# The turning ahead of the second half's rows, at 3 units of the schedule for a tile instead of 5.5

## The chip, the cores and the metric

The kernel runs on one core of one Trainium2 chip. The metric is the device time of one execution in microseconds (us), as the median of three runs. One core has five engines with queues of their own: PE (matrix products), DVE and ACT (vector and scalar work on tiles of 128 partitions), POOL (a second vector engine) and SP, which here only issues DMAs. Each engine works through its own instructions in the order in which the program was built; an instruction waits at the head of its queue until what it needs is there.

## The reference

One layer of a decoder trunk, for a prompt of 2048 tokens of width 1024 and eight single tokens with states of their own:

- rows are normalised by their root mean square and modulated by a learned scale and shift, `hn = rmsnorm(x) * (1 + scale) + shift`;
- one projection `z = hn @ w_in` yields the columns of two groups of heads;
- the first group (RG-LRU) runs a convolution of width 4, two block-diagonal gates, and a linear recurrence along the tokens, times `silu(za)`;
- the second (GLA, 4 heads) runs gated linear attention in chunks, a norm for each head, times `silu(zg)`;
- both are joined, projected by `w_out`, gated, added to `x`, and normalised once more.

The result is the output rows and the new states. All is float32; the kernel writes an operand as a high and a low part (`hh`, `hl` for the activations) and sums three products, so each projection of 1024 inputs is 24 matmuls (8 steps of lines L683, L684, L685).

## The kernel before, in words

The prompt is worked in two halves of 1024 tokens. In the first half the kernel projects and processes the heads of both groups; meanwhile it prepares what the second half needs, so that this work lies beside the matmuls. One such preparation is `turn_ahead` (L245 to L269). For each of the 8 tiles of 128 rows of the second half it

1. loads the rows to a tile `x` (SP, L248);
2. sums their squares (ACT, L166, called `squares`);
3. takes the root in 12 small steps on DVE (`scales`, lines L148 to L154) and multiplies the rows by it (`times`, L182, DVE);
4. turns the tile in blocks of 32x32 into a second tile `w` (DVE, L257);
5. stores `w` to a scratch in DRAM, `xtd` (SP, L261), and goes on to the next tile.

`x` and `w` are both tiles named `xt`, of which two slots exist. The rows come back later through `hn_load` (L271, DMAs at L281): group 0 (256 tokens) to two more tiles `xt`, groups 1 to 3 to `xst`. `modulate` (L188) then makes the new `hh` and `hl` from them: ACT at L201, DVE at L203, POOL at L204 for the high part, DVE at L205 for the low one. `modulate` runs bit by bit between the last matmuls of the first half.

The order is written by a small scheduler. `tick(u)` advances a clock by u units, where the main program calls it after each projection (one unit is a projection of 512 tokens, 24 matmuls); `after(u, f)` asks for f to be called when u more units have passed. What f issues then stands at that place in each engine's queue. The framework that builds the program gives out the slots of tiles and sets the semaphores by the order in which instructions come.

Behind the first half stands `gates_ahead` (L1662), the first user of the new rows. It loads two tiles of weights `w_6208` and `w_6210` (L315, 1 MB each) and projects with each of them tokens 0 to 255, then 256 to 511, then 512 to 1023 of the new half; the results go to PSUM tiles `acc`, of which there are four slots. A result leaves PSUM by ACT at L1152 (a sigmoid) and DVE at L1153, and then its slot is free. In the same stretch the last gate products of the recurrence stand (L1338 to L1340, `acc_6359` and `acc_6364`), and on DVE the sums of blocks for a seven-product scheme (`sums`, L1512, L1515, L1516, L1521).

Other names: `on` is the output of an attention head, which DVE scales at L1112 (four pieces) before PE transposes it at L1186; `vl` at L980 is the low part of a head's values, and frees the PSUM tile it reads; L1090 to L1098 are the products of an attention chunk; L327 on DVE splits weights.

Of the kernel before, what the change touches and what calls it, by code (L numbers as in the profile page):

```python
# [54 lines left out]
def hybrid_kernel(ctx, tc, i, o):  # L55
    nc = tc.nc
    V, S, G, PE, SP = nc.vector, nc.scalar, nc.gpsimd, nc.tensor, nc.sync
# [110 lines left out]
    def squares(pool, xt, m=P, tag="f512", ss=None, j0=0):  # L168
        if ss is None:
            ss = pool.tile([P, 4], F32, tag="ss", name="ss", bufs=2)  # L170
        for j, x in enumerate(xt, j0):
            square_sum(pool, ss[:m, j:j + 1], x[:m], m, D, tag)
        return ss

    def scales(pool, ss, n, m=P):
        rs = pool.tile([P, 4], F32, tag="rs", name="rs", bufs=2)
        rsqrt(pool, rs[:m, :n], ss[:m, :n], n, m, 1.0 / D)
        return rs

    def times(xt, rs, m=P, j0=0):  # L180
        for j, x in enumerate(xt, j0):
            V.tensor_scalar(x[:m], x[:m], rs[:m, j:j + 1], None, op0=OP.mult)  # L182
# [62 lines left out]
    def turn_ahead(q):  # L245

        x, w = [xp.tile([P, TH + NS], F32, tag="xt", name="xt")[:, :D] for _ in range(2)]
        SP.dma_start(x, i["x_prompt"][0, TH + q * P:TH + (q + 1) * P])  # L248

        def scaled(ss):  # L250
            with behind(V):
                times([x], scales(xp, ss, 1))
            after(0.5, turned)

        def turned():
            with behind(V):
                V.transpose(w.rearrange("p (c k j) -> p c k j", c=4, k=KT), x.rearrange("p (k c j) -> p c k j", c=4, k=KT))  # L257
            after(0.5, stored)

        def stored():  # L260
            SP.dma_start(xtd[q], w)  # L261
            if q < 7:
                after(1, lambda: turn_ahead(q + 1))

        def squared():
            ss = squares(xp, [x])
            after(0.5, lambda: scaled(ss))

        after(3, squared)  # L269

    def hn_load(g):  # L271

# [430 lines left out]
    def behind(q):  # L703

        return tc.issue_after(next(x for x in reversed(list(nc.cur_bb.bb.instructions)) if x.engine == q.engine))
# [17 lines left out]
    def after(units, fn, gla=False, val=False):  # L723
        clock[1] += 1
        heapq.heappush(pend, (clock[0] + units, clock[1], fn, gla, val))
# [17 lines left out]
    def ada_gate():  # L743

        pg = acc()

        def step(kt):
            ws = [xp.tile([P, TH + NS], F32, tag="xt", name="xt")[:, :D] for _ in range(2)]
            for n, w in enumerate(ws):
                SP.dma_start(w, i["w_ada"][0, (kt + n) * P:(kt + n + 1) * P, 2 * D:])  # L750

            def mm():
                for n in (1, 0):
                    for g in range(4):
                        PE.matmul(pg[32 * g:32 * g + 32, :256], sc[:, kt + n], ws[n][:, g * 256:(g + 1) * 256],
                                  start=kt == 0 and n == 1, stop=kt == KT - 2 and n == 0)
                if kt + 2 < KT:
                    step(kt + 2)
                else:
                    gr = xp.tile([P, 512], F32, tag="f512", name="gr")[:, :256]  # L760
                    S.copy(gr, pg[:, :256])
                    SP.dma_start(gated, gr)
                    after(4, lambda: ready("gate"))
                    turn_ahead(0)
            after(3, mm)

        step(0)
# [1512 lines left out]
```

## Time and profile before

| | |
|---|---|
| median of 3 runs | 1453.05 us (1452.84 to 1454.38) |
| the profiled execution | 1451.16 us, span 1449.4 us |
| mean granted TensorE clock | 0.993 |
| instructions | 23539 |
| PE busy | 1412.9 us, 97% of the span |
| DVE, ACT, POOL busy | 1064.7, 693.2, 221.1 us |
| the 8 turns L257 on DVE | 225.1 to 571.3 us, 1.24 us each |
| the 8 stores L261 on SP | 226.3 to 572.5 us |

Times inside the profile are counted from the start of the span. A row of a timeline gives the start, the duration, the engine, the line, the operation and its tiles; a figure in brackets is the idle time of that engine ahead of the row, with what ended it. Matmuls are pipelined, so the distance of two starts, and not the duration of one, is the pace.

### The profile page before, as it was taken

Reading aid. Unit: us, or ns where it says so; the run is one execution under the profiler, and the core shown is the slowest. Engines: PE = TensorE matmul, PEld = TensorE weight load, DVE = VectorE, ACT = ScalarE, POOL = GpSimd, SP = SyncE. Lnnn points to the kernel's source line nnn. Section 1 sums busy time; section 2 is a strip of 40 time slices with the busy share of each in tenths; the row PEclk is TensorE's granted clock in tenths of the full one; section 3 lists DMA queues with packets and bytes.
Section 4 is the critical chain, followed back from the end, with each engine's and each line's share of the span. In section 5 each row is a group of like instructions: output and inputs, shape, how many; then the busy total and the mean of one; then the engine's idle time right before and its main releaser. Section 6 shows DMA issues by size and latency. Waiting matters only on the chain.

```text
span 1449.4 us, 23539 instructions
## 1 busy us (share of the span) xinstructions
PE 1412.9 (97%) x8677; PEld 1244.8 (86%) x8677; DVE 1064.7 (73%) x2529; ACT 693.2 (48%) x1259; POOL 221.1 (15%) x366
## 2 busy tenths in 40 slices
PE   7999999999999998899999999999999999999998
PEld 6889989888898987788899999999998887778886
DVE  5757668777777687945448688596888986688886
ACT  4644544563456357624444554535567522144342
POOL 1200111122121113200110432333210000000000
PEclk9999999999999999899999999999999999999999
DMA  9755776875676646677744675665671767694453
GB/s 331 265 185 175 263 246 220 285 263 185 199 241 219 220 169 190 212 247 237 280 165 148 203 247 163 231 198 187 239 253 68 283 227 276 223 356 139 137 166 116
DMA packets 166424, 313.71 MB, mean 216 GB/s; under 512 B 13410, under 2 KB 94978, under 8 KB 163869
## 3 DMA queue, kind: packets, MB, share of 16 engines
q1 hardware_dynamic: 112405, 225.78, 45.9%
q0 software_dynamic: 22912, 70.96, 14.2%
q10 hardware_dynamic: 30992, 15.47, 3.6%
q8 instruction: 68, 1.11, 0.3%
q14 instruction: 47, 0.39, 0.1%
HBM read 192.70 MB, written 119.52 MB: 215 GB/s over the span
## 4 chain that ended last, share of the span: by engine, by line
PE 82%; DVE 6%; issue 4%; ACT 4%; DMA 3%; POOL 1%; SPq 0%; DVEq 0%; ACTq 0%; POOLq 0%
PE acc L1866 12%; PE acc L683 11%; PE acc L685 11%; PE acc L684 11%; PE tp L1866 9%; PE acc L1580 6%; PE acc L368 3%; PE acc L369 3%; PE acc L370 3%; PE po L1095 2%; PE acc L1338 1%; PE tp L1064 1%; DMA twd<-th 1%; PE acc L1340 1%; PE acc L1339 1%
## 5 line engine op out<-in xcount | busy, mean ns | idle before, releaser
L683 PE MATMUL acc<-hh,w 128*128 128x512 f32 (+3 forms) x1112 | 378.1, 340 | 14.1 <-DVE fs L203 12.5
L684 PE MATMUL acc<-hl,w 128*128 128x512 f32 (+3 forms) x1112 | 376.0, 338 | 0.0
L685 PE MATMUL acc<-hh,w 128*128 128x512 f32 (+3 forms) x1112 | 376.0, 338 | 0.0
L683 PEld LDWEIGHTS acc<-hh,w 128*128 128x128 f32 x1112 | 210.4, 189 | 31.4 <-DVE fs L203 12.6
L685 PEld LDWEIGHTS acc<-hh,w 128*128 128x128 f32 x1112 | 210.3, 189 | 16.2
L684 PEld LDWEIGHTS acc<-hl,w 128*128 128x128 f32 x1112 | 210.5, 189 | 15.0
L1866 PE MATMUL acc<-w,a 128*128 128x512 f32 (+1 forms) x792 | 184.9, 387 | 0.0
L1866 PEld LDWEIGHTS acc<-w,a 128*128 128x128 f32 x792 | 146.8, 188 | 33.3 <-issue 3.4
L368 PE MATMUL acc<-w,hh 128*128 128x256 f32 (+1 forms) x508 | 144.0, 283 | 1.1 <-DVE rs_y L150 0.8
L370 PE MATMUL acc<-w,hl 128*128 128x256 f32 (+1 forms) x508 | 142.7, 281 | 0.2 <-DVE hl L228 0.2
L369 PE MATMUL acc<-w,hh 128*128 128x256 f32 (+1 forms) x508 | 142.6, 281 | 0.0
L1866 PE MATMUL tp<-w,a 128*128 128x512 f32 x564 | 136.2, 391 | 0.0
L1866 PEld LDWEIGHTS tp<-w,a 128*128 128x128 f32 x564 | 105.2, 188 | 27.0 <-issue 5.2
L368 PEld LDWEIGHTS acc<-w,hh 128*128 128x128 f32 x508 | 95.5, 188 | 2.8 <-DVE rs_y L150 1.0
L370 PEld LDWEIGHTS acc<-w,hl 128*128 128x128 f32 x508 | 96.0, 189 | 0.4 <-DVE hl L228 0.4
L369 PEld LDWEIGHTS acc<-w,hh 128*128 128x128 f32 x508 | 95.5, 188 | 0.2
L1152 ACT ACTIVATE zs<-acc 128x512 f32<-128x512 f32 (+3 forms) x70 | 34.3, 490 | 102.8 <-PE acc L685 98.3
L1716 ACT CAST a<-s 128x512 fp32r<-128x512 f32 x61 | 36.5, 620 | 94.4 <-issue 33.7
L1301 DVE SCALAR_TENSOR_TENSOR cv<-xa,vecT,cv 128x512 f32<-128x512 f32 (+2 forms) x120 | 76.9, 643 | 4.1 <-ACT cv L1299 3.6
L1153 DVE SCALAR_TENSOR_TENSOR zs<-zs,acc 128x512 f32<-128x512 f32 (+3 forms) x70 | 38.4, 549 | 42.0 <-ACT zs L1152 42.0
L979 ACT CAST vh<-acc 128x256 fp32r<-128x256 f32 x56 | 20.4, 370 | 85.7 <-PE acc L370 61.6
L980 DVE TENSOR_TENSOR vl<-acc,vh 128x256 fp32r<-128x256 f32 x56 | 23.2, 418 | 42.8 <-ACT vh L979 42.7
(402 smaller groups left out, 2750.8 us busy)
## 6 DMA issues: line engine op xcount, KB each, us to landing
parts<-w SPq DMA_DIRECT2D x37, 1024.0 KB
w<-parts SPq DMA_DIRECT2D x28, 1024.0 KB
wr<-in_w_in_dram SPq DMA_DIRECT2D x38, 512.0 KB
a<-mixd SPq DMA_DIRECT2D x63, 256.0 KB
w<-wd SPq DMA_DIRECT2D x12, 1024.0 KB
w<-twd SPq DMA_DIRECT2D x20, 512.0 KB
wada<-in_w_ada_dram SPq DMA_DIRECT2D x16, 512.0 KB
mixd<-zs ACTq DMA_DIRECT2D x32, 256.0 KB
```

Of the source, the lines that this page charges most:

```text
L368: PE.matmul(ps, hh[:, kt, c], hi[:, kt % 4], start=kt == 0, stop=False)
L369: PE.matmul(ps, hh[:, kt, c], lo[:, kt % 4], start=False, stop=False)
L370: PE.matmul(ps, hl[:, kt, c], hi[:, kt % 4], start=False, stop=kt == KT - 1)
L683: PE.matmul(ps[:, :n], hi[:, kt], a, start=kt == 0, stop=False)
L684: PE.matmul(ps[:, :n], hi[:, kt], b, start=False, stop=False)
L685: PE.matmul(ps[:, :n], lo[:, kt], a, start=False, stop=kt == KT - 1)
L1152: S.activation(z, ps, AF.Tanh, scale=0.5)
L1153: V.scalar_tensor_tensor(z, z, 1.0, ps, op0=OP.add, op1=OP.mult)
L1301: V.scalar_tensor_tensor(cv[:, cq], xa[:, cq.start + k:cq.stop + k], cw[k], cv[:, cq], op0=OP.mult, op1=OP.add)
L1580: PE.matmul(ps, w[:, u, k], x[v][k], start=start and (k, u, v) == (0, 0, 0), stop=(k, u) == (3, 1), skip_group_check=True)
L1716: S.copy(t[:, 0, k], (low(t) if src is None else src)[:, k])
L1866: PE.matmul(ps, t[:, u, k], w[:, v, k, c], start=(q < 3 or ps is own) and (k, u, v) == (0, 0, 0), stop=(k, u) == (3, 1), skip_group_check= ...
```

## The change

The schedule of `turn_ahead` is packed. Three units after the load become two. Scaling and turn, which were two entries of the schedule half a unit apart, become one. The next tile's load follows directly on the store instead of one unit later. A tile takes 2 + 0.5 + 0.5 = 3 units and not 3 + 0.5 + 0.5 + 0.5 + 1 = 5.5. No instruction is added or taken away.

```diff
         def scaled(ss):
             with behind(V):
                 times([x], scales(xp, ss, 1))
-            after(0.5, turned)
-
-        def turned():
-            with behind(V):
                 V.transpose(w.rearrange("p (c k j) -> p c k j", c=4, k=KT), x.rearrange("p (k c j) -> p c k j", c=4, k=KT))
             after(0.5, stored)
 
         def stored():
             SP.dma_start(xtd[q], w)
             if q < 7:
-                after(1, lambda: turn_ahead(q + 1))
+                turn_ahead(q + 1)
...
-        after(3, squared)
+        after(2, squared)
```

The changed file is four lines shorter behind this place, so a line L683 of before is L679 there, and the turn L257 is L253, the store L261 is L257, the load L281 is L277. Buffer numbers differ as well.

The first place is the queue of SP before `gates_ahead`. Before, the store of the eighth tile (L261) stands between the loads of `xst` and ahead of the weights `w_6210`:

```order
L315 DMA w_6208<-parts_1199 128x2x1024
L1390 DMA wg_6602<-parts_1513 128x512
L281 DMA xst_6009<-xtd_70 32x8x256 x3
L281 DMA xt_5477<-xtd_70 32x4x256 x4
L281 DMA xst_6009<-xtd_70 32x8x256
L281 DMA xst_6010<-xtd_70 32x8x256 x2
L261 DMA xtd_70<-xt_5370 128x1024
L281 DMA xst_6010<-xtd_70 32x8x256 x2
L281 DMA xst_6011<-xtd_70 32x8x256 x4
L315 DMA w_6210<-parts_1206 128x2x1024
```

With the change the same stretch reads:

```order
L340 DMA parts_6000<-w_5995 256x1x1024
L311 DMA w_6208<-parts_1199 128x2x1024
L1386 DMA wg_6602<-parts_1513 128x512
L277 DMA xst_6009<-xtd_70 32x8x256 x4
L277 DMA xst_6010<-xtd_70 32x8x256 x4
L277 DMA xst_6011<-xtd_70 32x8x256 x4
L311 DMA w_6210<-parts_1206 128x2x1024
L1664 DMA zgd_69<-zs_6245 128x256
```

The eighth store and both tiles `xt` of group 0 have moved out of it, to a place some 30 rows earlier; the twelve loads of `xst` stand in one row, and `w_6210` behind them.

The second place is DVE in the third attention head, around the scaling L1112 that PE's transposes wait for (before at 355 us of the profile). Before, no piece of a turn is near:

```order
L1153 SCALAR_TENSOR_TENSOR zs_3986<-zs_3986,acc_3987 128x256
L153 SCALAR_TENSOR_TENSOR rs_t_3948<-rs_t_3948,rs_x_3949 128x4
L154 SCALAR_TENSOR_TENSOR ors_3946<-rs_t_3948,rs_y_3947 128x4
L1112 TENSOR_SCALAR on_3732<-on_3732,ors_3946 128x256 x4
L1153 SCALAR_TENSOR_TENSOR zs_3986<-zs_3986,acc_4014 128x256
```

With the change the seventh tile's scaling (L182) and turn (L253) stand there, and the last small steps of the head's own root, `ors`, behind them:

```order
L1149 SCALAR_TENSOR_TENSOR zs_4060<-zs_4060,acc_4061 128x256
L182 TENSOR_SCALAR xt_3846<-xt_3846,rs_3988 128x1024
L153 SCALAR_TENSOR_TENSOR rs_t_4022<-rs_t_4022,rs_x_4023 128x4
L253 STREAM_TRANSPOSE xt_3847<-xt_3846 128x1024
L154 SCALAR_TENSOR_TENSOR rs_y_4021<-rs_t_4022,rs_y_4021 128x4
L152 TENSOR_TENSOR rs_t_4022<-rs_y_4021 128x4
L153 SCALAR_TENSOR_TENSOR rs_t_4022<-rs_t_4022,rs_x_4023 128x4
L154 SCALAR_TENSOR_TENSOR ors_4020<-rs_t_4022,rs_y_4021 128x4
L1149 SCALAR_TENSOR_TENSOR zs_4060<-zs_4060,acc_4088 128x256
L1108 TENSOR_SCALAR on_3803<-on_3803,ors_4020 128x256 x4
```

The scaling of `on` has moved behind the next eviction. On PE, the order has moved too: the transposes L1186 (now L1182) that stood ahead of the attention chunk L1090 to L1098 now stand behind it and one further matmul.

The third place is DVE in the values of that head (before at 309 us). Before, the scaling, the turn and then the low part of the values follow each other:

```order
L154 SCALAR_TENSOR_TENSOR rs_3440<-rs_t_3442,rs_y_3441 128x1
L182 TENSOR_SCALAR xt_3202<-xt_3202,rs_3440 128x1024
L257 STREAM_TRANSPOSE xt_3203<-xt_3202 128x1024
L980 TENSOR_TENSOR vl_3322<-acc_3513,vh_3320 128x256
L980 TENSOR_TENSOR vl_3322<-acc_3540,vh_3320 128x256
L327 TENSOR_TENSOR w_3604<-wr_3605,w_3604 128x1024
```

With the change another tile's scaling and turn stand at the same place, but one `vl` between them:

```order
L154 SCALAR_TENSOR_TENSOR rs_3544<-rs_t_3546,rs_y_3545 128x1
L182 TENSOR_SCALAR xt_3327<-xt_3327,rs_3544 128x1024
L976 TENSOR_TENSOR vl_3372<-acc_3562,vh_3370 128x256
L253 STREAM_TRANSPOSE xt_3328<-xt_3327 128x1024
L976 TENSOR_TENSOR vl_3372<-acc_3593,vh_3370 128x256
L323 TENSOR_TENSOR w_3654<-wr_3655,w_3654 128x1024
```

The first `vl` has moved ahead of the turn.

## The prediction

> **What bounds the kernel now.** I read the page's busy times first, then the waits of PE, then the timelines around the longest wait.
>
> ```profile
> span 1449.4 us, 23539 instructions
> PE 1412.9 (97%) x8677; PEld 1244.8 (86%) x8677; DVE 1064.7 (73%) x2529; ACT 693.2 (48%) x1259; POOL 221.1 (15%) x366
> ```
>
> PE is busy for 97% of the span and idle for 36.5 us. Only idle PE time, or PE at a lower clock, can change. The list of who waited for whom (in total, times, longest) shows a third of it in one row:
>
> ```profile
> PE acc L683 <- DVE fs L203: 12.5, 1, 12.5
> ...
> PE acc L683 <- DVE vl L980: 1.4, 1, 1.4
> ```
>
> The second row, the short one, also lies beside a turn. The long wait, from the timelines of PE, DVE and SP (start, duration, engine, line):
>
> ```profile
> 573.72 0.28 PE L685 MATMUL acc<-hh,w 128*128 128x256 f32 x1
> 586.45 0.55 PE L683 MATMUL acc<-hh,w 128*128 128x256 f32 x1 [12.46 <-DVE fs L203]
> ...
> 571.28 1.23 DVE L257 STREAM_TRANSPOSE xt<-xt 128x1024 f32<-128x1024 f32 x1
> ...
> 572.54 0.34 SPq L261 DMA_DIRECT2D xtd<-xt x1
> 572.93 4.47 SPq L281 DMA_DIRECT2D xst<-xtd x6
> 577.50 0.56 SPq L315 DMA_DIRECT2D w<-parts x1
> ```
>
> PE ends the first product of `gates_ahead` (`w_6208`) at 574.00 and starts the second at 586.45. The row names DVE, but by the order this matmul is the first that reads `w_6210`, whose load SP issues only at 577.50. SP's queue explains that: the load stands behind six loads of `xst`, these behind the store of the eighth tile at 572.54, and that store behind the turn at 571.28. The turn was late since it wanted the second slot of `xt`, in which group 0 was loaded and modulated first. So the longest wait of the kernel is the change's target, 8.95 us from issue to first use included.
>
> PE's clock suffers too. By stages (length, busy PE, PEld, DVE, ACT, POOL, then the granted clock, DMA share, GB/s):
>
> ```profile
> 577.00:578.00 1.00, 0.00 (x0) 0.00 (x0) 0.84 (x2) 0.00 (x0) 0.00 (x0) 1.00 0.64 121
> 578.00:579.00 1.00, 0.00 (x0) 0.00 (x0) 0.00 (x0) 0.55 (x2) 0.00 (x0) 0.64 1.07 238
> ...
> 591.00:592.00 1.00, 1.00 (x7) 1.00 (x6) 1.00 (x2) 0.91 (x2) 0.00 (x0) 0.54 1.04 406
> ```
>
> The clock halves 0.28 us into the second row, at 578.28, which is 4.3 us after PE fell idle. It is back at 591.92, 5.5 us after PE resumed. Those 5.5 us did the work of 2.7.
>
> **The change part by part.** *The late store and the wait.* With the change the eighth store is done before 400 us, and no store stands in that stretch of SP's queue. `w_6210` then waits for its slot only, which a product ending at 564.3 frees:
>
> ```profile
> 564.36 0.59 ACT L1417 COPY xa<-acc 128x512 f32<-128x512 f32 x1 [1.30 <-PE acc L685]
> ```
>
> 564.4 + 8.95 = 573.3, just in time for 573.84. Taken alone this would give 12.46 us and 2.7 of clock back. What is late next must be asked: the tiles `acc` have four slots, so `acc_6364`, the second group at L1338, takes the slot of `acc_6249`, which DVE frees at L1153 for `zs_6282`, and `acc_6383` takes that of `acc_6286`, freed at L1153 for `zs_6319`. On DVE these stand behind all of `modulate` for groups 2 and 3 and the first `sums`, in the same order as before. The chain, ACT then DVE then PE:
>
> ```profile
> 575.89 0.38 ACT L1152 ACTIVATE zs<-acc 128x256 f32<-128x256 f32 x1
> 578.45 2.08 ACT L201 ACTIVATE ra<-xst,Sh,Gm 128x256 f32<-128x256 f32 x4 [2.18 <-issue]
> ...
> 594.05 0.41 DVE L1153 SCALAR_TENSOR_TENSOR zs<-zs,acc 128x256 f32<-128x256 f32 x1
> ...
> 597.79 0.41 DVE L1153 SCALAR_TENSOR_TENSOR zs<-zs,acc 128x256 f32<-128x256 f32 x1
> ...
> 597.45 0.28 PE L685 MATMUL acc<-hh,w 128*128 128x256 f32 x1
> 597.57 0.40 PE L1338 MATMUL acc<-xh,wg 128*128 128x512 f32 x1
> ...
> 598.96 0.39 PE L683 MATMUL acc<-hh,w 128*128 128x512 f32 x1
> ...
> 599.64 0.39 PE L683 MATMUL acc<-hh,w 128*128 128x512 f32 x1
> ```
>
> Before, group 2 started on ACT at 578.45. It waited for `xst`, whose loads stood behind the store. Now those loads go out early, and group 2 starts when ACT has evicted `zs_6245`, a product that PE ends at 574.00: with that eviction's 0.38, a little of it overlapped, at 574.32. So the chain moves forward by 578.45 - 574.32 = 4.13 us and no more; L203 and L205 on DVE and L204 on POOL feed each other as before. So `zs_6282` is out at 594.46 - 4.13 = 590.33 and `zs_6319` at 598.20 - 4.13 = 594.07. PE, without its wait, would be done with the four short products much sooner: 3 x 24 matmuls at 0.12 us (597.45 to 597.57) from 573.84 end at 582.5, the first group of L1338 at 583.2. There it waits 7.1 us for `zs_6282`, works 1.4 us, and waits 2.4 us for `zs_6319`. `acc_6383` starts at 594.07 where it started at 598.96: 4.89 us sooner, not 12.46.
>
> And the clock is lost again. An idle time of 7.1 us is over the 4.3 seen, so `acc_6383` starts at half rate. I charge the same 5.5 us as before, 2.7 us lost (the 1.4 us of work between the two waits I count for nothing). Before, the same loss lay ahead of 592, inside the 4.89. This stage: 4.89 - 2.7 = 2.2 us gained; bounds 4.9 (the clock stays up) and 1.4 (the work between the two waits delays the clock's return by its own 1.4 us, so 6.9 us pass at half rate).
>
> [...]
>
> A later `w_6210` costs nothing up to some 7 us, since PE then idles before it and not behind it.
>
> *The pieces moved on DVE.* Per tile they are twelve small steps of the root (0.16 us each, the row of 308.39 below), L182 and the turn; they go from places spread over 216 to 571 us to places within 200 to 395. In the two stretches, by windows:
>
> ```profile
> 190.00:420.00 230.00, 227.54 (x1321) 200.81 (x1320) 175.47 (x417) 116.91 (x204) 42.00 (x71) 1.00 0.70 233
> 420.00:572.00 152.00, 152.00 (x848) 133.01 (x848) 113.05 (x249) 82.05 (x138) 28.93 (x49) 1.00 0.61 199
> ```
>
> The relief from 420 on is worth nothing: PE is never idle there. In the first stretch PE idles 2.5 us and DVE has 54.5 us free. What counts is where PE waits for DVE within a microsecond or two. The places, from the timelines of DVE and PE:
>
> ```profile
> 308.39 0.16 DVE L154 SCALAR_TENSOR_TENSOR rs<-rs_t,rs_y 128x1 f32<-128x1 f32 x1
> 308.58 0.75 DVE L182 TENSOR_SCALAR xt<-xt,rs 128x1024 f32<-128x1024 f32 x1
> 309.37 1.25 DVE L257 STREAM_TRANSPOSE xt<-xt 128x1024 f32<-128x1024 f32 x1
> 310.54 0.72 DVE L980 TENSOR_TENSOR vl<-acc,vh 128x256 fp32r<-128x256 f32 x2
> ...
> 310.98 0.50 PE L683 MATMUL acc<-hh,w 128*128 128x512 f32 x1 [1.40 <-DVE vl L980]
> ...
> 249.02 1.50 DVE L1112 TENSOR_SCALAR on<-on,ors 128x256 f32<-128x256 f32 x4
> ...
> 251.13 1.23 DVE L327 TENSOR_TENSOR w<-wr,w 128x1024 fp32r<-128x1024 f32 x1
> ...
> 252.57 1.03 PE L1186 MATMUL tp<-ident,on 128*128 128x128 f32 x8
> ...
> 355.32 1.15 DVE L1112 TENSOR_SCALAR on<-on,ors 128x256 f32<-128x256 f32 x4
> 357.49 0.42 DVE L1153 SCALAR_TENSOR_TENSOR zs<-zs,acc 128x256 f32<-128x256 f32 x1 [1.02 <-ACT zs L1152]
> ...
> 356.87 1.03 PE L1186 MATMUL tp<-ident,on 128*128 128x128 f32 x8
> ...
> 357.66 0.36 PE L1090 MATMUL pkv<-vh,kTh 128*128 128x256 f32 x1
> ...
> 358.88 0.28 PE L683 MATMUL acc<-hh,w 128*128 128x256 f32 x1
> ...
> 223.86 0.41 DVE L1153 SCALAR_TENSOR_TENSOR zs<-zs,acc 128x256 f32<-128x256 f32 x1
> ...
> 224.12 0.28 PE L683 MATMUL acc<-hh,w 128*128 128x256 f32 x1
> ```
>
> At 310.98 PE waited 1.40 us for a `vl` behind the turn. Now it stands ahead of it, and is out some 1.2 us sooner: -1.2 (bounds -1.4 and 0).
>
> At 252.57 PE had 3.2 us in hand on the first piece of L1112. By the order a root, L182, the turn and the weight split L327 now come first: 0.75 + 1.25 + 1.23 = 3.2 us, and some 0.4 for what of the root isn't overlapped. So L1112 starts near 252.6 and its last piece ends near 253.9: +0.7 (bounds 0 and 1.9, the latter with all twelve steps of the root at 0.16).
>
> At 356.87 L1112 now follows the eviction at 357.49, so its first piece is out at 358.2. But on PE the attention chunk and a matmul, 358.88 + 0.12 - 357.66 = 1.34 us, now come before the transposes, which puts these at 358.2 as well: 0 (bounds 0 and 2.2, with L182, the turn and the steps in full).
>
> At 224 us PE's transposes move forward, to 224.24 behind one matmul, and L1112 no longer stands behind the turn but behind the eviction at 223.86, with its first piece at about 224.4: +0.2 (0 to 0.6). Other places have slack of several microseconds, or PSUM slots between. Eight squares on ACT, eight loads and seven stores on SP only change places; ACT is busy for half of that stretch, and no wait of PE there names it: 0. An `x` has now two units, 10.9 us, to land before its squares (24 matmuls a unit, three of them in 598.96 to 599.64), more than the 8.95 that 1 MB took above, with half the size: 0. POOL's queue is not passed by anything.
>
> Sum: -2.2 - 1.2 + 0.7 + 0 + 0.2 = -2.5 us. The profiled execution took 1451.16 us, so 1448.7; it lies 1.89 below the median of the runs, so I forecast a median of 1450.5.
>
> **The rivals.** I call a change of 0.2%, 2.9 us, what a measurement of this kernel tells from none.
>
> *The clock costs nothing behind the new wait.* The two waits are cut by work, or PE warms sooner than at 586. Then the stage gives 4.9 and the sum is -5.2: 1447.9. Against it stands that 7.1 us is well over 4.3.
>
> *The full stall comes back.* If the sums or evictions move forward with PE, all of 12.46 + 2.7 + 0.3 = 15.5 us is gained: 1437.6. Against it: the eviction of `zs_6282` stands behind four modulations and three sums on DVE in one fixed order, and these behind ACT's start at 574.32.
>
> *DVE makes PE wait early, and the kernel is slower.* The packed turns push L1112 back at 224, 252 and 357 us in full: 0.6 + 1.9 + 2.2 = 4.7, the 1.2 at 310.98 doesn't come, and the stage gives its lower end of 1.4: +3.3, that is 1456.4. It decides from early waits of 2.9 us beyond what the late stage gives. For it speaks that DVE is already busy for 76% of that stretch; against it, that two of the three places were costed near 0 by the order.
>
> *The store stays late.* That the eighth turn still waits for a slot: 1453. The order excludes it nearly, since group 0 is loaded behind the eighth store.
>
> **How the numbers follow.** My case has 0.61; its own range is 1448 to 1453.5, and near half of it lies below 1450.15, the bound of faster. The clock without price has 0.14, nearly all of it faster; the full stall 0.06; slower by early waits 0.14, mostly beyond 1455.95; no effect 0.05. Faster: 0.27 + 0.12 + 0.06 = 0.45. Slower: 0.13. Same: the rest, 0.42. The range from 1446.0 to 1455.5 leaves out the full stall and the worst of the early waits.
>
> **What would show it.** In the profile after: no wait of 12 us at L683; in its place 5 to 8 us at the second group of L1338, with DVE `zs` L1153 as releaser, and 1 to 3 us at the 512-wide L683 behind it; a granted clock of 0.5 over some 5 us from there; group 2 at L201 starting some 4 us earlier against the end of the first short product. At 311 the wait of 1.4 nearly gone, at 252 a new one below 1 us at L1186, none at 357. I am wrong if PE waits at L1186 or L1064 for several microseconds between 200 and 400, if L1338 doesn't wait, or if the clock there stays at 1.

## The result, and the profile after

The changed kernel takes 1461.10 us in the median of four runs (1459.87 to 1463.06), beside 1453.08 us before: a ratio of 1.0055 with a 95% interval of 1.0037 to 1.0072. It is 8.0 us slower. The forecast was 1450.5 us, with a range from 1446.0 to 1455.5.

The list of PE's waits of the changed kernel (line and releaser, then us in total, times, longest):

```profile
PE tp L1060 <- DVE xb L1045: 7.9, 2, 6.9
PE acc L1334 <- DVE zs L1149: 3.8, 2, 2.5
PE acc L679 <- DVE zs L1149: 2.9, 1, 2.9
PE acc L679 <- DMA w<-parts: 2.8, 1, 2.8
...
PE acc L679 <- DVE vl L976: 0.4, 1, 0.4
```

The wait of 12.46 us is gone. In its place stand the second to fourth row, 2.5 + 2.9 + 2.8 us (of the second row only the longer of the two waits lies there). The wait for `vl` fell from 1.4 to 0.4. The first row is new: 6.9 us at the transposes L1060, which waited nowhere for more than 1.0 us before.

Where the time went can be read from the starts of the same matmuls in the two profiles:

| matmul | before | after | behind by |
|---|---|---|---|
| first decay product (L995, now L991), ahead of everything that the change touches | 56.31 | 57.48 | 1.17 |
| last attention chunk before 250 us (L1090, now L1086) | 241.74 | 243.27 | 1.53 |
| decay product of the third head, first | 309.19 | 310.97 | 1.78 |
| the same, second | 322.00 | 322.79 | 0.79 |
| next attention chunk | 329.22 | 339.11 | 9.89 |
| end of the product of `w_6208`, first in `gates_ahead` | 574.00 | 584.22 | 10.22 |
| first of the seven products (L1580, now L1576) | 609.84 | 617.16 | 7.32 |
| span | 1449.4 | 1458.1 | 8.7 |

9.1 us are lost between 323 and 339 us, and 2.9 are won in `gates_ahead`. The first 1.17 us arise before the change can act (the first tile's squares stand at 201 us), and the last 1.4 come after 617 us; for neither was a cause found.

The loss in the timelines of PE, ACT, DVE and SP of the changed kernel:

```profile
323.02 0.39 PE L679 MATMUL acc<-hh,w 128*128 128x512 f32 x1
330.81 2.07 PE L1060 MATMUL tp<-xb,e 128*128 128x128 f32 x8 [6.94 <-DVE xb L1045]
...
314.38 0.63 ACT L998 ACTIVATE e<-e 128x512 f32<-128x512 f32 x1
321.83 1.06 ACT L166 ACTIVATE junk<-xt 128x1024 bf16<-128x1024 f32 x1 [6.81 <-DMA xt<-in_x_prompt_dram]
323.00 1.28 ACT L999 ACT_TABLE_LOAD   x1
324.29 0.63 ACT L999 ACTIVATE e<-e 128x512 f32<-128x512 f32 x1
...
311.61 1.24 DVE L253 STREAM_TRANSPOSE xt<-xt 128x1024 f32<-128x1024 f32 x1
324.95 0.69 DVE L1000 TENSOR_TENSOR xb<-xb,e 128x512 f32<-128x512 f32 x1 [8.54 <-ACT e L999]
...
330.07 0.68 DVE L1045 SCALAR_TENSOR_TENSOR xb<-acc,xb 128x512 f32<-128x512 f32 x1
...
312.88 0.33 SPq L257 DMA_DIRECT2D xtd<-xt x1
313.25 0.42 SPq L248 DMA_DIRECT2D xt<-in_x_prompt_dram x1
```

The sixth tile's rows are asked for at 313.25, directly behind the fifth tile's store, and are there at 321.8, 8.6 us later. The sum of their squares (L166 with `xt`) stands on ACT between the two functions of a head's decay, L998 (exponential) and L999 (logarithm), and waits for them from 315.0 on. Behind it stand L999, the scan of the decay on DVE and `xb` at L1045, for which PE's transposes wait. The same places in the kernel before, on ACT and PE:

```profile
312.59 0.63 ACT L1002 ACTIVATE e<-e 128x512 f32<-128x512 f32 x1
313.24 1.28 ACT L1003 ACT_TABLE_LOAD   x1
...
326.62 1.06 ACT L166 ACTIVATE junk<-xt 128x1024 bf16<-128x1024 f32 x1
...
323.00 1.16 PE L1064 MATMUL tp<-xb,e 128*128 128x128 f32 x8
```

There L1003, the counterpart of L999, began at 313.24 with its table and had no square ahead of it; the square stood behind the second decay, at 326.62, and waited for nothing.

The clock made it worse. By stages of the changed kernel (columns as in the prediction's rows; the granted clock is the first figure behind the five engines):

```profile
326.00:328.00 2.00, 0.00 (x0) 0.00 (x0) 1.97 (x9) 0.43 (x2) 0.00 (x0) 1.00 1.10 366
328.00:330.00 2.00, 0.00 (x0) 0.00 (x0) 1.30 (x3) 1.76 (x3) 0.00 (x0) 0.59 0.73 221
330.00:332.00 2.00, 1.19 (x5) 1.19 (x6) 1.42 (x3) 1.95 (x3) 0.00 (x0) 0.50 0.07 22
332.00:334.00 2.00, 2.00 (x11) 1.90 (x10) 1.07 (x2) 0.89 (x3) 0.00 (x0) 0.50 0.00 0
334.00:336.00 2.00, 2.00 (x8) 1.60 (x7) 1.83 (x6) 1.98 (x3) 0.00 (x0) 0.70 0.00 0
```

PE falls idle at 330.81 - 6.94 = 323.87. The clock halves at 328.4, 4.5 us later, and is back at 335.2, 4.4 us after PE resumed: 4.4 us at half rate are 2.2 us lost. 6.94 + 2.2 is the whole 9.1.

And the stage that the forecast was about, in the timelines of PE, ACT and SP of the changed kernel, with the longest wait of the loads L277 from SP's list of waits between 550 and 590 us:

```profile
587.04 0.35 PE L679 MATMUL acc<-hh,w 128*128 128x256 f32 x1 [2.82 <-DMA w<-parts]
600.55 0.50 PE L1334 MATMUL acc<-xh,wg 128*128 128x512 f32 x1 [2.47 <-DVE zs L1149]
604.38 0.77 PE L679 MATMUL acc<-hh,w 128*128 128x512 f32 x1 [2.86 <-DVE zs L1149]
...
584.54 2.06 ACT L201 ACTIVATE ra<-xst,Sh,Gm 128x256 f32<-128x256 f32 x4
...
558.66 21.92 SPq L277 DMA_DIRECT2D xst<-xtd x12
580.67 0.55 SPq L311 DMA_DIRECT2D w<-parts x1
...
SPq L277 <- DMA mixd<-zs: 9.0, 2, 8.6
```

PE ends the product of `w_6208` at 587.04 - 2.82 = 584.22. Group 2 starts on ACT at 584.54, 0.32 us behind that, as the forecast had it. `w_6210` goes out only at 580.67: the loads of `xst` stand ahead of it, and one of them waited 8.6 us for a store from `zs` to `mixd`.

From the end of `w_6208` to the 512-wide product it was 598.96 - 574.00 = 24.96 us before and is 604.38 - 584.22 = 20.16 now, 4.80 us shorter.

### The profile page after: what moved, and what is told of

Read it like the earlier page. It is cut to its first block, busy times and chain, and to the rows that moved or that the text cites. A ratio compares the mean times of both kernels' runs of the same rounds, so it can differ in the third digit from the quotient of the medians.

```text
span 1458.1 us, 23543 instructions
## 1 busy us (share of the span) xinstructions
PE 1420.3 (97%) x8677; PEld 1249.5 (86%) x8677; DVE 1062.8 (73%) x2529; ACT 692.9 (48%) x1259; POOL 220.8 (15%) x366
## 4 chain that ended last, share of the span: by engine, by line
PE 77%; issue 7%; DVE 7%; DMA 4%; ACT 4%; POOL 1%; DVEq 0%; SPq 0%; POOLq 0%; ACTq 0%
PE acc L1862 12%; PE acc L679 10%; PE acc L681 10%; PE acc L680 10%; PE tp L1862 9%; PE acc L1576 6%; PE acc L364 3%; PE acc L365 3%; PE acc L366 3%; PE po L1091 1%; DMA twd<-th 1%; PE acc L1334 1%; PE tp L1060 1%; PE tp L1182 1%; PE acc L1336 1%
## 5 line engine op out<-in xcount | busy, mean ns | idle before, releaser
L679 PE MATMUL acc<-hh,w 128*128 128x512 f32 (+3 forms) x1112 | 379.1, 341 | 6.5 <-DVE zs L1149 2.9
L679 PEld LDWEIGHTS acc<-hh,w 128*128 128x128 f32 x1112 | 210.8, 190 | 24.6 <-issue 4.1
L976 DVE TENSOR_TENSOR vl<-acc,vh 128x256 fp32r<-128x256 f32 x56 | 23.4, 420 | 48.5 <-ACT vh L975 48.5
```

The costliest lines, as they stand in the source:

```text
L679: PE.matmul(ps[:, :n], hi[:, kt], a, start=kt == 0, stop=False)
```

## The experiments

Two theories stood against each other for the loss: that a square on ACT waits for its rows and holds up the decay behind it, or that the turns, packed closer, keep DVE from what PE waits for.

**The sixth tile's squares over other rows.**

```diff
-            ss = squares(xp, [x])
+            ss = squares(xp, [hh[:, 0, :D].bitcast(F32) if q == 5 else x])
```

The kernel leaves out the sum over this tile's own rows, so these rows are scaled by a wrong root.

> The changed kernel, but the sum of squares of the sixth tile is taken over another tile that is long there (1024 columns of hh, so the rows of that tile are scaled by a wrong root); the other engines keep their order word for word, and on ACT this one square stands some dozen rows earlier, out of the middle of the decay's Abs-Exp-Ln chain, and waits for no load. Theory (the square on ACT waits for the rows' load and holds up the decay behind it): the wait of 6.94 us at L1060 is gone and so is the half clock behind it, 9.1 us between the second L991 and the next L1086; the time falls from 1461.1 to about 1452. Rival (the turns, packed closer on DVE, are what makes PE late): DVE's order is unchanged, so 5 us or more of the wait stay, and the time stays above 1458.

1450.31 us (1449.27 to 1453.01), a ratio to the kernel before of 0.998 (0.997 to 0.9989). That is 10.8 us below the changed kernel, by moving one square on ACT, which now stands at 302.33, with the order on PE, DVE, POOL and SP unchanged. PE's list of waits now begins with `gates_ahead`:

```profile
PE acc L1334 <- DVE zs L1149: 4.5, 2, 3.1
...
PE tp L1060 <- DVE xb L1045: 1.0, 1, 1.0
```

The second L991 and the next chunk L1086 stand at 323.13 and 330.36, 7.23 us apart as before (7.22). In this kernel another tile's square, the seventh, waits for its rows for 5.79 us on ACT, and no wait in PE's list follows from it: it is the place of the square, together with the landing, that costs. The theory of the square stands; the packing on DVE, which is the same in both kernels, is not the cause.

**One part of the change at a time.** The merge of scaling and turn alone:

```diff
                 times([x], scales(xp, ss, 1))
-            after(0.5, turned)
-
-        def turned():
-            with behind(V):
                 V.transpose(w.rearrange("p (c k j) -> p c k j", c=4, k=KT), x.rearrange("p (k c j) -> p c k j", c=4, k=KT))
```

> The kernel before with scaling and turn in one piece alone (5 units a tile). By the order the eighth store stands ahead of the first load of xt as in the changed kernel, and no square stands in a decay chain. Theory: the wait of 12.46 us at the second product of gates_ahead is gone, two waits of 2 to 3 us stand at L1334 and the 512-wide L679, nothing is lost at 310 to 340 us; about 3 us faster than before, 1450. Rival (denser DVE work costs): the tiles are spread over twice the time, so a few us are lost here and there all the same, and the gain is below 1 us.

1453.96 us (1451.78 to 1455.32), ratio 1.0005 (0.9996 to 1.0015): no change. The late part of the expectation came, as PE's list shows, but the gain went elsewhere:

```profile
PE acc L364 <- DVE vl L976: 4.1, 1, 4.1
PE acc L1334 <- DVE zs L1149: 3.4, 2, 2.1
PE acc L679 <- DMA w<-parts: 3.2, 1, 3.2
PE acc L679 <- DVE zs L1149: 2.9, 1, 2.9
```

The first row is a wait at the values of the third head. On DVE the eviction L976 stood behind a scan and other long steps:

```profile
298.73 2.29 DVE L1353 TENSOR_TENSOR_SCAN tg<-xl,tx 128x1024 f32<-128x1024 f32 x1
300.93 0.67 DVE L795 TENSOR_TENSOR tr<-tr 128x512 f32<-128x512 f32 x1
...
301.57 0.68 DVE L1371 SCALAR_TENSOR_TENSOR zs<-tg,zs 128x512 f32<-128x512 f32 x1
302.17 1.29 DVE L801 TENSOR_TENSOR tr<-tr,th 128x512 f32<-128x512 f32 x2
303.38 0.42 DVE L976 TENSOR_TENSOR vl<-acc,vh 128x256 fp32r<-128x256 f32 x1
...
303.85 0.58 PE L364 MATMUL acc<-w,hh 128*128 128x256 f32 x1 [4.06 <-DVE vl L976]
```

None of these is a piece of a turn. In the kernel before, an eviction of this kind (L980 at 300.42) stands directly ahead of that scan (L1357 at 300.76), and the wait isn't there. The order of DVE comes out of the scheduler, and moving the turns moved it. So the rival was right that a few microseconds go elsewhere. The rows point to the order rather than to the work of the turns, but the order was not tried on its own.

The missing pause alone (the load of the next tile directly behind the store):

```diff
-                after(1, lambda: turn_ahead(q + 1))
+                turn_ahead(q + 1)
```

> The kernel before without the unit between store and next load alone (4.5 units a tile); scaling and turn stay apart, three units before the squares. By the order the late store is gone and no square stands between Exp and Ln. Theory: as the merge alone, about 3 us faster than before, 1450. Rival: below 1 us.

1455.51 us (1454.30 to 1460.88), ratio 1.0019 (1.0007 to 1.0030): slower by 0.2%, where 3 us faster were expected. The 12.46 us are gone here too. A wait of 4.20 us for `vl` at L368, at the same place as in the merge alone, and one of 2.19 at L1064 at 329 us have come; their cause stays open.

The changed kernel with three units before the squares:

```diff
-        after(2, squared)
+        after(3, squared)
```

> The changed kernel with three units between load and squares, as before (4 units a tile). One square still stands between Exp and Ln of the same decay, but its load goes out earlier. Theory: only what is left of the load's 8.6 us is waited for; with the load out several us sooner the wait at L1060 is 0 to 3 us, and the time between 1450 and 1454. Rival (the place of the square counts, not its load): the wait stays near 7 us and the time at 1459 or more.

1459.32 us (1457.83 to 1460.41), ratio 1.0044 (1.0029 to 1.0059). The expectation failed, but not for the rival's reason. From the timelines of SP, ACT and PE:

```profile
313.41 0.43 SPq L248 DMA_DIRECT2D xt<-in_x_prompt_dram x1
...
321.04 1.06 ACT L166 ACTIVATE junk<-xt 128x1024 bf16<-128x1024 f32 x1 [6.43 <-DMA xt<-in_x_prompt_dram]
...
330.03 2.08 PE L1060 MATMUL tp<-xb,e 128*128 128x128 f32 x8 [5.97 <-DVE xb L1045]
```

With a unit more for each tile it is the fifth tile that stands here, and its load goes out at 313.41, not sooner than 313.25. So a unit more in the schedule bought no time at this place: the load still landed 7.6 us later, in the middle of the decay.

**The sixth tile later.** 3.5 units before the squares for that tile alone, 2 for the others.

```diff
-        after(2, squared)
+        after(3.5 if q == 5 else 2, squared)
```

> The changed kernel with 3.5 units between load and squares for the sixth tile alone; the result is the reference's. Its square leaves the decay chain between Exp and Ln for the place where the kernel before had one, behind the casts at L1066. Theory (the wait for the rows' load in the middle of the decay is the loss): as with the other rows, no wait at L1060 at 324 to 331 us, 9 us less than the changed kernel, about 1451, so 0.1 to 0.2% below the kernel before. Rival (any delay of the tiles costs elsewhere, as in the two variants that changed the order of DVE at the values): a wait of 3 us or more at another line between 290 and 400, and 1454 or more.

1451.03 us (1449.62 to 1451.88), ratio 0.9978 (0.9969 to 0.9987), 10 us below the changed kernel. ACT has the square behind the second decay again, and PE its transposes without a wait:

```profile
327.44 1.06 ACT L166 ACTIVATE junk<-xt 128x1024 bf16<-128x1024 f32 x1
...
323.82 1.16 PE L1060 MATMUL tp<-xb,e 128*128 128x128 f32 x8
```

This is the change as it was meant, but for the place of one tile's square, and it is worth 0.22%.

**What is left in `gates_ahead`.** The forecast had said that behind the removed wait PE would wait for two evictions, which stand behind the sums on DVE. On the kernel with the sixth tile later, the sums were pinned:

```diff
+            with tc.issue_after(evicted[k]):
+                step(n, u)
```

with `evicted` holding DVE's evictions of `gates_ahead` in their order, and `k` that of `zs_6282` for the first step of the sums and `zs_6319` for the second. PE's two waits in the kernel with the sixth tile later, which the pins are to remove:

```profile
591.16 0.80 PE L1334 MATMUL acc<-xh,wg 128*128 128x512 f32 x1 [4.81 <-DVE zs L1149]
...
594.99 0.77 PE L679 MATMUL acc<-hh,w 128*128 128x512 f32 x1 [2.18 <-DVE zs L1149]
```

> The same, and in gates_ahead the first step of the block sums is pinned behind the eviction of zs_6282 and the second behind that of zs_6319 on DVE, instead of ahead of them. Theory (behind the removed wait PE waits for these two evictions, which stand behind the sums): the waits of 2 to 3 us at L1334 and at the 512-wide L679 go or fall below 1.5 in total, the half clock behind them goes too; 5 to 6 us faster than the run beside it, about 1445. Rival (the chain of modulations on DVE is the bound, not the sums): the waits shrink by less than 1.5 us in total; or the sums, now later, make the first seven-product product wait at L1576, and the gain is given back.

1445.87 us (1444.43 to 1446.87), ratio 0.9944 (0.9930 to 0.9957), 5.2 us below the run beside it. The wait at L1334 in this stage, 4.81 us, is gone, and that at the 512-wide L679 fell from 2.18 to 1.85:

```profile
591.77 0.47 PE L679 MATMUL acc<-hh,w 128*128 128x512 f32 x1 [1.85 <-DVE zs L1149]
```

The sum of the two did not fall below 1.5 us as expected, but the time did as forecast. By the starts of the same matmuls the gain lies in this stage: from the end of the product of `w_6208` to the first of the seven products it is 608.35 - 574.83 = 33.52 us with the sixth tile later and 604.36 - 576.01 = 28.35 us with the pins, 5.17 us less. Half rate is left in the stage (the mean granted clock from 590 to 612 us rose from 0.77 to 0.92).

With both evictions ahead of the first step, and that of `zs_6356` ahead of the second:

> As the run that pinned the sums, but the first step of the sums is pinned behind the evictions of zs_6282 and zs_6319, and the second behind that of zs_6356. Theory (only the order of evictions and sums still holds PE): the wait of 1.8 us at the 512-wide L679 goes, no half clock is left between 585 and 612, and the time falls by some 2 us to 1444. Rival (the sums, pushed back again, make a product of the seven wait, or the start of the 512-wide product hangs on the last low part of the modulation as well): no gain, or the wait under another name.

1444.55 us (1443.68 to 1445.62), ratio 0.9939 (0.9925 to 0.9952): 1.3 us less than the last, of 2 expected, with the ranges of the two overlapping. Each against the runs of the kernel before that were made beside it, they are 9.0 and 8.2 us faster, so a gain over the last is not shown. The wait at the 512-wide L679 for `zs` is gone, and no half clock is left in the stage:

```profile
590.00:612.00 22.00, 19.99 (x86) 15.55 (x85) 19.19 (x21) 14.46 (x17) 1.57 (x2) 1.00 0.52 159
```

The rival came in part as well: from the end of the product of `w_6208` to the first of the seven products this kernel needs 24.22 us instead of 28.35, but among the seven products, where the last had no wait, PE now waits three times, for 1.0, 0.6 and 0.4 us, and by the starts 3.2 of the 4.1 us are lost again. This kernel has the lowest median of the study, 0.6% below the kernel before and 1.1% below the changed one.

The same pins, as in the first of the two, on the kernel before, with its schedule of the turns as it was:

> The kernel before, its schedule of the turns unchanged, with the first step of the sums pinned behind the eviction of zs_6282 and the second behind that of zs_6319. Theory (the evictions hold PE only once the late store is gone): the wait of 12.46 us at the second product of gates_ahead stays, the evictions come earlier without anyone waiting for them, and the time is that of the kernel before within 1.5 us. Rival (the sums' place is worth 5 us by itself): 1448.

1453.11 us (1451.54 to 1454.01), ratio 0.9996 (0.9988 to 1.0005), no change. The list of waits names now what before had to be concluded:

```profile
PE acc L683 <- DMA w<-parts: 12.2, 1, 12.2
```

The evictions are worth 5 us only where the late store is gone, and the store's removal is worth 3 us only where nothing else breaks.

## Why the prediction was wrong

The step that failed is the one that put eight squares, eight loads and seven stores at 0, with two arguments. "An `x` has now two units, 10.9 us, to land" took units of the schedule for time. Between the load at 313.25 and the square's turn on ACT at 315.0 lay 1.8 us. A unit is a count of projections in the order in which the program is written, not a time on an engine: the load stands on SP behind the fifth tile's store, and that behind the fifth turn, which DVE ended at 312.85. And the landing took 8.6 us for 512 KB, nearly as much as the 8.95 us for 1 MB, in a stretch with the DMA engines at a mean share of 0.88 (313 to 322 us). "ACT is busy for half of that stretch" was the wrong question: one square that waited held ACT's queue for 6.81 us, idle as ACT was. What counted was what stands behind it, and that was L999, on which a scan, `xb` and PE's transposes hang. The prediction followed this for DVE at four places and left ACT out. Instead of 0 this term is 9.1 us: 6.94 of waiting, 2.2 of half clock. The prediction had named the place among its signs of being wrong ("PE waits at L1186 or L1064 for several microseconds between 200 and 400"), but put no price on it by way of ACT.

Slower was forecast with a chance of 0.13, through DVE's late L1112. That mechanism was not what came: the list of the changed kernel has 0.6 us for L1108 (the old L1112), in two waits.

The other terms:

- The late wait. 4.89 us were forecast for the start of `acc_6383`, and 4.80 measured; the reason, evictions behind the sums on DVE, is shown by the run with the first pins. 7.1 us at L1334 and 2.4 at L679 were forecast as waits, and 2.82 + 2.47 at the load and at L1334, and 2.86 at L679, came. That `w_6210` would wait "for its slot only" was wrong: it stood behind the loads of `xst`, and these behind the store to `mixd`, until 580.67. That a late `w_6210` would cost nothing agrees with the 4.80 us, but was not tried on its own.
- The clock behind it. 2.7 us were charged, and 4.80 - 2.90 = 1.9 measured, as what is lost again until the first of the seven products (2.90 is 10.22 - 7.32 of the table). With it the stage gave 2.9 us and not 2.2.
- `vl` at 310 us: -1.2 forecast, -1.0 measured by the wait and by the starts (1.78 to 0.79).
- 252 us: +0.7 forecast; between the chunks at 243 us and the decay product at 310 it is 0.25 by the starts. 224 us: +0.2, and 0.24 between the chunks at 224.26 and 232.63. 357 us: 0 forecast, and 0.37 between the chunks at 351.91 and 374.90.

With that one square out of the decay the sum of -2.5 us is near what came: the kernel with the sixth tile later lies 3.07 us below the runs of the kernel before that were made beside it.

## What to carry to other kernels

A wait for a DMA held here what stood behind it on its engine (6.81 us on ACT became 9.1 on PE, while 5.79 us at another place were followed by no wait of PE), so when an instruction is moved in an order that a scheduler writes, look on each engine, however idle, at what stands directly behind it and who waits for that. Units of a schedule are no time: take the issue of the load and the turn of its reader from the order and the timeline, and set the landing time that a trace shows at that place (here 8.6 and 7.6 us for 512 KB) between them. Where a long wait is removed, look for what is late next and move that too; here the second step was worth more than the first (5.2 us and 3.1), and worth nothing alone.

## What the runs showed of the hardware

PE's clock halved also behind waits of 2.17 and 4.06 us. In the kernel with the first pins PE waited 2.17 us and resumed at 578.18, and the clock halved only after that:

```profile
578.00:580.00 2.00, 1.82 (x14) 1.85 (x15) 1.29 (x2) 2.00 (x5) 1.49 (x3) 0.90 0.59 176
580.00:582.00 2.00, 2.00 (x11) 2.00 (x11) 1.49 (x3) 2.00 (x5) 1.16 (x2) 0.50 0.32 112
582.00:584.00 2.00, 2.00 (x15) 2.00 (x15) 2.00 (x5) 0.72 (x2) 1.19 (x2) 0.75 0.01 4
```

By these rows the half rate lasts from about 579.6 to 583.0, 3.4 us that cost 1.7, and begins 3.6 us after PE fell idle at 576.01. The run with both evictions first has a wait of 2.52 us at the same matmul, up to 577.15, and no half rate behind it:

```profile
578.00:580.00 2.00, 2.00 (x19) 2.00 (x19) 1.46 (x2) 2.00 (x5) 1.65 (x2) 1.00 0.58 207
580.00:582.00 2.00, 2.00 (x19) 2.00 (x18) 2.00 (x5) 1.22 (x3) 0.56 (x1) 1.00 0.00 0
582.00:584.00 2.00, 2.00 (x19) 2.00 (x18) 2.00 (x4) 0.38 (x1) 2.00 (x4) 1.00 0.03 10
```

In the merge alone PE fell idle at 299.79, with a wait of 4.06 us, and the granted clock, 1.00 up to 302.0, was 0.50 from there, 2.2 us later. In these three waits and the 6.94 us of the changed kernel, the delay from idle to half rate, where it came, lies between 2.2 and 4.5 us. A wait of 2.17 us was followed by half rate that cost 1.7 us more in one run, one of 2.52 us by none in another.
